# Two-layer decoder trunk on one Trainium2 core: the up product's three terms as 256-column matmuls in one PSUM region per column group

## The chip, the cores and the metric

The kernel runs on one core of one Trainium2 chip. The metric is the time of one execution in device microseconds (us); the median over several runs is given. A core has a matrix engine (TensorE, in the profile PE for matmuls and PEld for weight loads), VectorE (DVE), ScalarE (ACT), GpSimd (POOL) and SyncE (SP), which here issues the transfers. Matmuls write into PSUM; the vector and scalar engines read it from there.

## The reference

The reference computes two layers on 256 tokens of width 2048, in float32. Layer 0 mixes with a gated convolution and a spatial gate, layer 1 with attention; each layer ends with a squared-ReLU MLP of hidden width 8192, which is what the change touches:

```
def rms_norm(x, g):
    y = xf * lax.rsqrt(jnp.mean(xf * xf, axis=-1, keepdims=True) + EPS)
    return (y * g.astype(jnp.float32)).astype(x.dtype)

def channel_mlp(h, w_up, w_down):
    a = jax.nn.relu(h @ w_up)
    return (a * a) @ w_down

    h = rms_norm(x, ffn_norm[layer])
    x = x + channel_mlp(h, w_up[layer], w_down[layer])
```

## The kernel before

All weights are read once, in chunks of 512 rows by 512 columns (four k steps of 128 rows each, 1 MB). `load_chunk` takes one chunk from HBM into a `raw` tile (three of them) and splits it in two halves into a rounded part `whi` (ScalarE, L60) and a remainder `wlo` (VectorE, L61), both in a 32-bit format that TensorE streams in one pass; five buffers of each hold half chunks of two k steps. Activations are split in the same way into a high and a low half that lie side by side in one tile, `[P, G, 2, T]`: for each k step 256 high columns (the tokens), then 256 low ones. A product is the sum of three terms, high x high, high x low and low x high.

In most products (`unit`, L87) the activations are the held operand of TensorE and 512 columns of weights are streamed; two PSUM tiles with the tag "acc" collect 128 tokens each. The up product of the MLP (`unit_t`) is turned round: 128 columns of weights are held and the tokens streamed, so that the result is already transposed for the down product. For each of four column groups `f` it has one PSUM tile `up` of 512 columns, two with the tag "acc" and two with the tag "tp" (four regions for each tag). Per k step it issues four matmuls with `whi` held that stream both halves of the activations, 512 columns (L101), and then four with `wlo` held that stream the high half alone, 256 columns, into the first half of the same tile (L104). A chunk is 4 k steps, a unit is 4 chunks, 16 k steps, and gives 512 hidden columns.

`up(j)` then evacuates: for each column group ScalarE copies the second half of the tile to `r` (L348), VectorE adds the first half (L349), squares with relu two groups at a time (L350), and `split` makes the two parts of the next activation `a` (L118 on ScalarE, L119 on VectorE). The activations `h` carry the norm's gain but not 1/rms; since relu and square let a positive factor per token through, the MLP multiplies its down product by `rstd2`, the square of 1/rms (L338), when it adds it to `x` (L370).

`mlp` runs 16 up units and 16 down units per layer, in the order of 5 up, 4 down, 4 up, 4 down, 4 up, 4 down, 3 up, 4 down. Each engine works through its instructions in program order, which a scheduler lays out over the engines; a transposition of the last block of `h` stands ahead of chunk 1 of the first up unit (`pending`).

Of the kernel before, what the change touches and what calls it, by code (L numbers as in the profile page):

```python
# [9 lines left out]
F32 = mybir.dt.float32  # L10
F32R = mybir.dt.float32r
I32 = mybir.dt.int32
AF = mybir.ActivationFunctionType
ALU = mybir.AluOpType
AX = mybir.AxisListType

P = 128
T = 256
NT = T // P
D = 2048  # L20
NB = 512
G = NB // P
# [10 lines left out]
def trunk_kernel(ctx: ExitStack, tc, x, xT, vecs, sgu_gain, wsT, w_in, w_mix, w_qkv, w_ao, w_up, w_dn, out):  # L33
    nc = tc.nc
    pool = lambda name, bufs=1, **kw: ctx.enter_context(tc.tile_pool(name=name, bufs=bufs, **kw))
    const = pool("const")
# [3 lines left out]
    work = pool("work", 2)  # L40
    small = pool("small", 4)
    psum = pool("psum", 4, space=bass.MemoryType.PSUM)
# [3 lines left out]
    idle = lambda: None  # L46
# [3 lines left out]
    def load_chunk(src, first=False):  # L50
        raw = first_raw if first else raws.tile([P, G, NB], F32, name="raw")
        if not first:
            nc.sync.dma_start(raw, src)
        got = []
        for h in range(2):
            hi = parts.tile([P, 2, NB], F32R, name="whi")
            lo = parts.tile([P, 2, NB], F32R, name="wlo")
            for a, b in ((0, 1), (1, 2)) if first else ((0, 2),):
                w = raw[:, 2 * h + a:2 * h + b]
                nc.scalar.activation(hi[:, a:b], w, AF.Copy)  # L60
                nc.vector.tensor_tensor(lo[:, a:b], w, hi[:, a:b].bitcast(F32), ALU.subtract)  # L61
            got += [(hi[:, 0], lo[:, 0]), (hi[:, 1], lo[:, 1])]
        return got

    def unit(acts_t, src, order=(0, 1, 2, 3), first=False, last=False, behind=()):

        ps = [psum.tile([P, NB], F32, name=f"acc{t}", tag="acc") for t in range(NT)]
        for n, c in enumerate(order):
            if callable(acts_t[c]):
                acts_t[c] = acts_t[c]()  # L70
            chunk = load_chunk(src[c], first and n == 0)
            for later in behind[n:n + 1]:
                later()
            if n == 1 and pending:
                pending.pop()()
            ahi, alo = parts_of(acts_t[c])
            if last and n == G - 1:
                steps = [(k, t, term) for t in range(NT) for k in range(G) for term in range(3)]
            else:

                steps = [(k, t, term) for k in range(G) for term in range(3) for t in range(NT)]
            for k, t, term in steps:
                hi, lo = chunk[k]
                held, streamed = ((ahi, hi), (ahi, lo), (alo, hi))[term]
                start = n == 0 and k == 0 and term == 0
                stop = n == G - 1 and k == G - 1 and term == 2
                nc.tensor.matmul(ps[t], held[:, k, t * P:(t + 1) * P], streamed, start=start, stop=stop)  # L87
        return ps

    def unit_t(acts_t, src):  # L90

        ps = [psum.tile([P, 2, T], F32, name=f"up{f}", tag="acc" if f < 2 else "tp") for f in range(G)]
        for c in range(G):
            chunk = load_chunk(src[c])
            if c == 1 and pending:
                pending.pop()()
            both = acts_t[c]
            for k, (hi, lo) in enumerate(chunk):
                start, stop = c == 0 and k == 0, c == G - 1 and k == G - 1
                for f in range(G):  # L100
                    nc.tensor.matmul(ps[f], hi[:, f * P:(f + 1) * P], both[:, k], start=start, stop=False,  # L101
                                     skip_group_check=True)
                for f in range(G):
                    nc.tensor.matmul(ps[f][:, 0], lo[:, f * P:(f + 1) * P], both[:, k, 0], start=False, stop=stop,  # L104
                                     skip_group_check=True)
        return ps

    def act_pair(tag):

        return acts.tile([P, G, 2, T], F32R, name=tag, tag=tag, bufs=4 if tag == "h" else 5)  # L110

    def parts_of(pair):
        return pair[:, :, 0], pair[:, :, 1]

    def split(pair, at, src):

        hi, lo = parts_of(pair)
        nc.scalar.activation(hi[at], src, AF.Copy)  # L118
        nc.vector.tensor_tensor(lo[at], src, hi[at].bitcast(F32), ALU.subtract)  # L119
# [6 lines left out]
    def tps():  # L126
        return psum.tile([P, NB], F32, name="tp", tag="tp")
# [21 lines left out]
    nc.scalar.dma_start(vec, vecs)  # L149
    ident = const.tile([P, P], F32, name="ident")  # L150
    make_identity(nc, ident)
    x_sb = [const.tile([P, D], F32, name=f"x{t}") for t in range(NT)]
    wsT_sb = work.tile([P, 8, P], F32, name="wsT_sb", tag="B", bufs=1)
    sg = work.tile([P, 1024], F32, name="sg", tag="A", bufs=1)
# [20 lines left out]
    def rstd_of(ss):  # L175
        v = small.tile([P, NT], F32, name="var")
        nc.vector.tensor_reduce(v, ss, AX.X, ALU.add)
        nc.vector.tensor_scalar(v, v, 1.0 / D, EPS, ALU.mult, ALU.add)
        return rsqrt_(v, NT, "rstd")

    def norm_block(hT, j, ss, gcol):
        stats(ss, j)
        pending.append(lambda: turn_block(hT, j, gcol))
# [42 lines left out]
    def new_ss():  # L226
        return small.tile([P, NT, NJ], F32, name="ss")


    def first_block(j):  # L230
        xt = acts.tile([P, G, T], F32, name="xt", tag="a", bufs=5)
        if j == 0:
            for k in range(G):
                nc.sync.dma_start(xt[:, k], xT[:, k])  # L234
                if k == 0:
                    nc.sync.dma_start(first_raw[:, 0], w_in[2][0][:, 0])
            for k in range(1, G):
                nc.sync.dma_start(first_raw[:, k], w_in[2][0][:, k])  # L238
        else:
            nc.sync.dma_start(xt, xT[:, j * G:(j + 1) * G])  # L240
        pair = act_pair("h")
        for k in range(G):
            g = C_MIXG + j * G + k
            split_scaled(pair, k, xt[:, k], vec[:, g:g + 1])
        return pair

    hT = [lambda j=j: first_block(j) for j in range(NJ)]
    mixed_in = [None] * 4
    tail = ()
    for half in range(2):  # L250
        ps_c = unit(hT, w_in[2 + half], first=half == 0, behind=tail)
        ps_x = unit(hT, w_in[4 + half], behind=[lambda j=j: load_x(j) for j in range(NJ)] if half == 0 else ())
        if half == 0:
# [4 lines left out]
            rstd = rstd_of(ss)  # L258
# [75 lines left out]
    def mlp(layer, hT, rstd, gcol):  # L334
        aT = {}

        rstd2 = small.tile([P, NT], F32, name="rstd2")
        nc.vector.tensor_tensor(rstd2, rstd, rstd, ALU.mult)  # L338

        def up(j):  # L340

            pair = act_pair("a")
            got = unit_t(hT, w_up[layer, j])
            for half in range(2):
                r = work.tile([P, 2, T], F32, name="r")
                for f in range(2):
                    ps = got[2 * half + f]
                    nc.scalar.activation(r[:, f], ps[:, 1], AF.Copy)  # L348
                    nc.vector.tensor_tensor(r[:, f], ps[:, 0], r[:, f], ALU.add)  # L349
                nc.vector.scalar_tensor_tensor(r, r, 0.0, r, ALU.max, ALU.mult)  # L350
                split(pair, (slice(None), slice(2 * half, 2 * half + 2)), r)
            aT[j] = pair

        ss = new_ss()
        nxt = [None] * NJ
        done = 0
        for s in range(4):
            while done < min(16, 4 * s + 5):
                up(done)
                done += 1  # L360
            for j in range(NJ):
                last = s == 3 and j == NJ - 1 and gcol is None
                ps = unit([aT[4 * s + c] for c in range(4)], w_dn[layer, s, j], last=last)
                for t in range(NT):

                    w = NB // 2 if last and t == NT - 1 else NB
                    for a in range(0, NB, w):
                        cols = slice(j * NB + a, j * NB + a + w)
                        xb = x_sb[t][:, cols]
                        nc.vector.scalar_tensor_tensor(xb, ps[t][:, a:a + w], rstd2[:, t:t + 1], xb, ALU.mult, ALU.add)  # L370
                        if s == 3 and gcol is None:
                            nc.sync.dma_start(out[t * P:(t + 1) * P, cols], xb)
                if s == 3 and gcol is not None:
                    norm_block(nxt, j, ss, gcol)
        return (nxt, rstd_of(ss)) if gcol is not None else None

    hT, rstd = project(mixed_in, w_mix, (0, 2, 1, 3), C_FFNG, tail)
    hT, rstd = mlp(0, hT, rstd, C_MIXG + 16)


# [86 lines left out]
    for hg in range(4):  # L467
        got = {}
# [18 lines left out]

    hT, rstd = project(oT, w_ao, (0, 1, 2, 3), C_FFNG + 16, tail)
    mlp(1, hT, rstd, None)


# [44 lines left out]
```

## Time and profile before

| | before |
|---|---|
| median of 3 runs | 2139.3 us (2139.08 to 2139.3) |
| profiled execution | 2139.24 us |
| its span, first to last instruction | 2137.5 us |
| TensorE matmuls busy, number | 2126.9 us, 10464 |
| VectorE busy, number | 1253.8 us, 1658 |
| ScalarE busy, number | 960.9 us, 1168 |

The span is what the profiler records of the program; the execution's own time has 1.7 us around it. A busy engine is one with an instruction under way; matmuls overlap, so the sum of their durations is longer than the time that they take.

### The profile page before, as it was taken

What the parts mean: (1) busy time and instruction counts of PE and PEld (TensorE: products, weight loads), DVE (VectorE), ACT (ScalarE), POOL (GpSimd) and SP (SyncE); (2) the same over time, 40 slices, a digit from 0 to 9 for tenths busy, and PEclk for the clock granted to TensorE, in tenths of its full rate; (3) what the DMA queues carried; (4) which work ended last, traced back from release to release, by engine and by line L of the source; (5) the groups of instructions that cost most, each with busy time, mean ns of one, the idle gap of its engine ahead of it and who ended that gap; (6) DMA issues with size and microseconds to landing.
All of it is one profiled execution on the core that took longest, in us unless ns stands there. A gap on an engine that the chain in (4) does not pass through costs nothing.

```text
span 2137.5 us, 25939 instructions
## 1 busy us (share of the span) xinstructions
PE 2126.9 (100%) x10464; PEld 1795.9 (84%) x10464; DVE 1253.8 (59%) x1658; ACT 960.9 (45%) x1168; POOL 3.1 (0%) x13
## 2 busy tenths in 40 slices
PE   8999999999999999999999999999999999999999
PEld 6888888888888888888888888888888888888887
DVE  6655666655564565565666667565655554564554
ACT  5444444443443453444454555444434443443442
POOL 0000000000000000000000000000000000000000
PEclk9999999999999999999999999999999999999999
DMA  8555555555555555555545445555555555555553
GB/s 323 192 193 180 186 187 182 193 187 193 191 185 191 195 185 191 196 187 187 185 170 179 166 167 177 177 178 194 180 197 195 183 194 197 180 194 195 182 204 128
DMA packets 58584, 403.34 MB, mean 189 GB/s; under 512 B 6624, under 2 KB 7392, under 8 KB 10464
## 3 DMA queue, kind: packets, MB, share of 16 engines
q1 hardware_dynamic: 58320, 401.63, 55.0%
q8 instruction: 82, 1.34, 0.3%
q14 instruction: 38, 0.31, 0.0%
q10 hardware_dynamic: 144, 0.05, 0.0%
HBM read 399.56 MB, written 2.10 MB: 188 GB/s over the span
## 4 chain that ended last, share of the span: by engine, by line
PE 99%; DMA 0%; SPq 0%; DVE 0%; ACT 0%; issue 0%; DVEq 0%
PE acc L87 63%; PE up L101 22%; PE up L104 11%; PE tp L207 1%; PE tp L192 0%; PE tp L425 0%; DMA raw<-in_w_in 0%; PE tp L458 0%; PE tp L445 0%; PE tp L307 0%; PE tp L459 0%; SPq L234 0%; SPq L238 0%; DVE wlo L61 0%; ACT whi L60 0%
## 5 line engine op out<-in xcount | busy, mean ns | idle before, releaser
L61 DVE TENSOR_TENSOR wlo<-raw,whi 128x1024 fp32r<-128x1024 f32 (+1 forms) x754 | 919.2, 1221 | 809.3 <-ACT whi L60 808.6
L60 ACT ACTIVATE whi<-raw 128x1024 fp32r<-128x1024 f32 (+1 forms) x754 | 796.7, 1058 | 1108.3 <-PE acc L87 702.4
L87 PE MATMUL acc<-whi,a 128*128 128x512 f32 x2560 | 690.0, 390 | 0.0
L87 PEld LDWEIGHTS acc<-whi,a 128*128 128x128 f32 x2560 | 479.1, 188 | 98.2
L101 PE MATMUL up<-h,whi 128*128 128x512 f32 x2048 | 559.0, 394 | 0.0
L87 PE MATMUL acc<-wlo,a 128*128 128x512 f32 x1280 | 395.0, 389 | 0.0
L87 PE MATMUL acc<-whi,h 128*128 128x512 f32 x1408 | 386.6, 393 | 6.2 <-ACT whi L60 6.2
L101 PEld LDWEIGHTS up<-h,whi 128*128 128x128 f32 x2048 | 350.5, 189 | 47.5
L104 PEld LDWEIGHTS up<-h,wlo 128*128 128x128 f32 x2048 | 314.3, 189 | 43.6
L104 PE MATMUL up<-h,wlo 128*128 128x256 f32 x2048 | 325.8, 281 | 0.0
L87 PEld LDWEIGHTS acc<-whi,h 128*128 128x128 f32 x1408 | 263.8, 189 | 60.8 <-ACT whi L60 7.4
L87 PEld LDWEIGHTS acc<-wlo,a 128*128 128x128 f32 x1280 | 240.3, 188 | 50.4
L87 PE MATMUL acc<-wlo,h 128*128 128x512 f32 x704 | 218.3, 391 | 0.5 <-DVE wlo L61 0.5
L87 PEld LDWEIGHTS acc<-wlo,h 128*128 128x128 f32 x704 | 132.6, 188 | 28.9 <-DVE wlo L61 1.4
L370 DVE SCALAR_TENSOR_TENSOR x<-acc,rstd,x 128x512 f32<-128x512 f32 (+1 forms) x65 | 45.3, 739 | 15.8 <-PE acc L87 15.5
L349 DVE TENSOR_TENSOR r<-up,r 128x256 f32<-128x256 f32 x128 | 47.7, 414 | 0.0
L119 DVE TENSOR_TENSOR a<-r,a 128x512 fp32r<-128x512 f32 x64 | 43.7, 683 | 0.0
L350 DVE SCALAR_TENSOR_TENSOR r<-r 128x512 f32<-128x512 f32 x64 | 43.5, 680 | 0.0
L118 ACT ACTIVATE a<-r 128x512 fp32r<-128x512 f32 x64 | 39.9, 623 | 1.8
L348 ACT ACTIVATE r<-up 128x256 f32<-128x256 f32 x128 | 37.9, 380 | 0.0
L222 ACT ACTIVATE gc<-acc,rstd 128x512 f32<-128x512 f32 x28 | 17.8, 686 | 23.0 <-PE acc L87 18.6
L123 ACT ACTIVATE h<-tp,vec 128x256 fp32r<-128x256 f32 x48 | 20.5, 469 | 12.4 <-DVE h L124 12.4
(80 smaller groups left out, 383.4 us busy)
## 6 DMA issues: line engine op xcount, KB each, us to landing
raw<-in_w_up SPq DMA_DIRECT2D x128, 1024.0 KB, 4.8
raw<-in_w_dn SPq DMA_DIRECT2D x128, 1024.0 KB, 4.8
raw<-in_w_qkv SPq DMA_DIRECT2D x48, 1024.0 KB, 4.8
raw<-in_w_in SPq DMA_DIRECT2D x39, 1024.0 KB, 4.9
raw<-in_w_mix SPq DMA_DIRECT2D x16, 1024.0 KB, 4.8
raw<-in_w_ao SPq DMA_DIRECT2D x16, 1024.0 KB, 4.8
x<-in_x SPq DMA_DIRECT2D x8, 256.0 KB, 8.6
out_dram<-x SPq DMA_DIRECT2D x7, 256.0 KB, 6.1
```

Source lines behind the costliest of these rows:

```text
L60: nc.scalar.activation(hi[:, a:b], w, AF.Copy)
L61: nc.vector.tensor_tensor(lo[:, a:b], w, hi[:, a:b].bitcast(F32), ALU.subtract)
L87: nc.tensor.matmul(ps[t], held[:, k, t * P:(t + 1) * P], streamed, start=start, stop=stop)
L101: nc.tensor.matmul(ps[f], hi[:, f * P:(f + 1) * P], both[:, k], start=start, stop=False, skip_group_check=True)
L104: nc.tensor.matmul(ps[f][:, 0], lo[:, f * P:(f + 1) * P], both[:, k, 0], start=False, stop=stop, skip_group_check=True)
L118: nc.scalar.activation(hi[at], src, AF.Copy)
L119: nc.vector.tensor_tensor(lo[at], src, hi[at].bitcast(F32), ALU.subtract)
L207: nc.tensor.transpose(tp[:, i * T + t * P:i * T + (t + 1) * P], src[t][:, c:c + P], ident)
L348: nc.scalar.activation(r[:, f], ps[:, 1], AF.Copy)
L349: nc.vector.tensor_tensor(r[:, f], ps[:, 0], r[:, f], ALU.add)
L350: nc.vector.scalar_tensor_tensor(r, r, 0.0, r, ALU.max, ALU.mult)
L370: nc.vector.scalar_tensor_tensor(xb, ps[t][:, a:a + w], rstd2[:, t:t + 1], xb, ALU.mult, ALU.add)
```

## The change

Per k step the up product now issues twelve matmuls of 256 columns: `whi` held with the high half streamed, `whi` held with the low half, `wlo` held with the high half, each for the four column groups. All three terms of a column group add up in one region of 256 columns, and two groups share a PSUM tile, so a unit has two tiles with the tag "acc" and none with the tag "tp". VectorE reads a tile from PSUM once, applies relu and multiplies each column by the token's 1/rms (`rows`); ScalarE squares; `split` stays. The down product is then added to `x` without a factor. For `rows`, 1/rms has to lie along the columns in all 128 partitions: `spread` makes it once per layer, ahead of chunk 2 of the first up unit, with two copies on VectorE, two matmuls with the identity and a copy by ScalarE.

```diff
-    def unit_t(acts_t, src):
+    def unit_t(acts_t, src, behind=()):
-        ps = [psum.tile([P, 2, T], F32, name=f"up{f}", tag="acc" if f < 2 else "tp") for f in range(G)]
+        ps = [psum.tile([P, 2, T], F32, name=f"up{i}", tag="acc") for i in range(2)]
         for c in range(G):
             chunk = load_chunk(src[c])
+            for later in behind[c:c + 1]:
+                later()
             if c == 1 and pending:
                 pending.pop()()
-            both = acts_t[c]
+            xhi, xlo = parts_of(acts_t[c])
             for k, (hi, lo) in enumerate(chunk):
-                start, stop = c == 0 and k == 0, c == G - 1 and k == G - 1
-                for f in range(G):
-                    nc.tensor.matmul(ps[f], hi[:, f * P:(f + 1) * P], both[:, k], start=start, stop=False,
-                                     skip_group_check=True)
-                for f in range(G):
-                    nc.tensor.matmul(ps[f][:, 0], lo[:, f * P:(f + 1) * P], both[:, k, 0], start=False, stop=stop,
-                                     skip_group_check=True)
+                for term in range(3):
+                    held, streamed = ((hi, xhi), (hi, xlo), (lo, xhi))[term]
+                    start = c == 0 and k == 0 and term == 0
+                    stop = c == G - 1 and k == G - 1 and term == 2
+                    for f in range(G):
+                        nc.tensor.matmul(ps[f // 2][:, f % 2], held[:, f * P:(f + 1) * P], streamed[:, k],
+                                         start=start and f % 2 == 0, stop=stop, skip_group_check=True)
...
-        rstd2 = small.tile([P, NT], F32, name="rstd2")
-        nc.vector.tensor_tensor(rstd2, rstd, rstd, ALU.mult)
+        rows = work.tile([P, T], F32, name="rows", tag="C", bufs=1)
+        def spread():
+            tp = tps()
+            for t in range(NT):
+                held = work.tile([P, P], F32, name="held", tag="qT")
+                nc.vector.tensor_scalar(held, ones, rstd[:, t:t + 1], None, ALU.mult)
+                nc.tensor.matmul(tp[:, t * P:(t + 1) * P], held, ident, start=True, stop=True)
+            nc.scalar.activation(rows, tp[:, :T], AF.Copy)
...
-            got = unit_t(hT, w_up[layer, j])
+            got = unit_t(hT, w_up[layer, j], (idle, idle, spread) if j == 0 else ())
             for half in range(2):
                 r = work.tile([P, 2, T], F32, name="r")
-                for f in range(2):
-                    ps = got[2 * half + f]
-                    nc.scalar.activation(r[:, f], ps[:, 1], AF.Copy)
-                    nc.vector.tensor_tensor(r[:, f], ps[:, 0], r[:, f], ALU.add)
-                nc.vector.scalar_tensor_tensor(r, r, 0.0, r, ALU.max, ALU.mult)
+                nc.vector.scalar_tensor_tensor(r, got[half], 0.0, rows.unsqueeze(1).broadcast_to([P, 2, T]),
+                                               ALU.max, ALU.mult)
+                nc.scalar.activation(r, r, AF.Square)
                 split(pair, (slice(None), slice(2 * half, 2 * half + 2)), r)
...
-                        nc.vector.scalar_tensor_tensor(xb, ps[t][:, a:a + w], rstd2[:, t:t + 1], xb, ALU.mult, ALU.add)
+                        nc.vector.tensor_tensor(xb, ps[t][:, a:a + w], xb, ALU.add)
```

On TensorE the first k step of the first up unit stood like this before (`up_2472` to `up_2475` are the four column groups' tiles):

```order
L101 MATMUL up_2472<-h,whi 128x512
L101 MATMUL up_2473<-h,whi 128x512
L101 MATMUL up_2474<-h,whi 128x512
L101 MATMUL up_2475<-h,whi 128x512
L104 MATMUL up_2472<-h,wlo 128x256
L104 MATMUL up_2473<-h,wlo 128x256
L104 MATMUL up_2474<-h,wlo 128x256
L104 MATMUL up_2475<-h,wlo 128x256
```

After the change the same k step is this (`up_2473` and `up_2474` are the two tiles, of two column groups each; x2 are two equal rows, the two groups):

```order
L107 MATMUL up_2473<-h,whi 128x256 x2
L107 MATMUL up_2474<-h,whi 128x256 x2
L107 MATMUL up_2473<-h,whi 128x256 x2
L107 MATMUL up_2474<-h,whi 128x256 x2
L107 MATMUL up_2473<-h,wlo 128x256 x2
L107 MATMUL up_2474<-h,wlo 128x256 x2
```

Eight matmuls have become twelve, and none of 512 columns is left among them.

On ScalarE the evacuation of the first up unit stood like this before, in the midst of the conversions `whi`, with the transposed last block of `h` (L123) ahead of them:

```order
L123 ACTIVATE h<-tp,vec 128x256 x4
L60 ACTIVATE whi<-raw 128x1024 x6
L348 ACTIVATE r<-up_2472 128x256
L348 ACTIVATE r<-up_2473 128x256
L348 ACTIVATE r<-up_2474 128x256
L348 ACTIVATE r<-up_2475 128x256
L60 ACTIVATE whi<-raw 128x1024
L118 ACTIVATE a<-r 128x2x256
L60 ACTIVATE whi<-raw 128x1024
L118 ACTIVATE a<-r 128x2x256
```

Now it is this (L126 is the former L123, L121 the former L118):

```order
L126 ACTIVATE h<-tp,vec 128x256 x4
L60 ACTIVATE whi<-raw 128x1024 x2
L351 ACTIVATE rows<-tp 128x256
L60 ACTIVATE whi<-raw 128x1024 x4
L361 ACTIVATE r<-r 128x512
L121 ACTIVATE a<-r 128x2x256
L361 ACTIVATE r<-r 128x512
L121 ACTIVATE a<-r 128x2x256
L60 ACTIVATE whi<-raw 128x1024 x8
```

The copy of `rows` stands two conversions after the block of `h`, and the four operations of the evacuation stand together, ahead of the next conversion, where the conversions stood between them before.

On VectorE the start of the MLP now has the two copies among the splits of the last block of `h` (L127), ahead of five `wlo`, and then the two readings of PSUM:

```order
L143 SCALAR_TENSOR_TENSOR rstd<-rstda,rstd 128x2
L127 SCALAR_TENSOR_TENSOR h<-tp,vec,h 128x256 x2
L349 TENSOR_SCALAR held<-ones,rstd 128x128
L127 SCALAR_TENSOR_TENSOR h<-tp,vec,h 128x256 x2
L349 TENSOR_SCALAR held<-ones,rstd 128x128
L61 TENSOR_TENSOR wlo<-raw,whi 128x1024 x5
L359 SCALAR_TENSOR_TENSOR r<-up_2473,rows 128x512
L359 SCALAR_TENSOR_TENSOR r<-up_2474,rows 128x512
```

Before, the square of 1/rms (L338) stood there in place of the copies, and six `wlo` and six operations of 256 and 512 columns in place of the five and two.

## Rows read from the trace of the kernel before

**Rows 1.** The page, parts 1 and 2: engine totals, TensorE's clock by slice.

```profile
PE 2126.9 (100%) x10464; PEld 1795.9 (84%) x10464; DVE 1253.8 (59%) x1658; ACT 960.9 (45%) x1168; POOL 3.1 (0%) x13
...
PEclk9999999999999999999999999999999999999999
```

**Rows 2.** The page, part 4: the chain that ended last, shares by engine.

```profile
PE 99%; DMA 0%; SPq 0%; DVE 0%; ACT 0%; issue 0%; DVEq 0%
```

**Rows 3.** The chain in order of time: start, duration (us), what.

```profile
by line: PE acc L87 62.9%; PE up L101 22.3%; PE up L104 11.3%; PE tp L207 0.6%; PE tp L192 0.5%; PE tp L425 0.5%; DMA raw<-in_w_in 0.4%; PE tp L458 0.4%; PE tp L445 0.2%; PE tp L307 0.2%; PE tp L459 0.2%; SPq L234 0.1%; SPq L238 0.1%; DVE w
...
110.49 1.78 PE tp L307 x16
...
440.27 87.07 PE acc L87 x384
617.12 87.09 PE acc L87 x384
```

**Rows 4.** Timeline of PE, 526.9 to 531.5 us: down unit to up unit.

```profile
527.17 1.07 PE L101 MATMUL up<-h,whi 128*128 128x512 f32 x4
528.08 0.64 PE L104 MATMUL up<-h,wlo 128*128 128x256 f32 x4
528.55 1.09 PE L101 MATMUL up<-h,whi 128*128 128x512 f32 x4
529.48 0.63 PE L104 MATMUL up<-h,wlo 128*128 128x256 f32 x4
529.95 1.09 PE L101 MATMUL up<-h,whi 128*128 128x512 f32 x4
```

**Rows 5.** Timeline of PE, 326.9 to 340 us: the MLP's first up unit.

```profile
327.00 1.07 PE L101 MATMUL up<-h,whi 128*128 128x512 f32 x4
327.91 0.64 PE L104 MATMUL up<-h,wlo 128*128 128x256 f32 x4
...
333.38 1.17 PE L101 MATMUL up<-h,whi 128*128 128x512 f32 x4
334.39 0.63 PE L104 MATMUL up<-h,wlo 128*128 128x256 f32 x4
...
339.06 1.09 PE L101 MATMUL up<-h,whi 128*128 128x512 f32 x4
```

**Rows 6.** Timeline of DVE, 318 to 341 us: 1/rms and what follows.

```profile
335.25 0.15 DVE L140 SCALAR_TENSOR_TENSOR rstd<-rstda,rstd 128x2 f32<-128x2 f32 x1
...
335.71 0.15 DVE L338 TENSOR_TENSOR rstd<-rstd 128x2 f32<-128x2 f32 x1
```

**Rows 7.** Timeline of ACT, 336 to 366 us: end of the first up unit.

```profile
350.98 1.18 ACT L348 ACTIVATE r<-up 128x256 f32<-128x256 f32 x4
352.82 1.06 ACT L60 ACTIVATE whi<-raw 128x1024 fp32r<-128x1024 f32 x1 [0.66 <-PE up L101]
...
358.49 1.06 ACT L60 ACTIVATE whi<-raw 128x1024 fp32r<-128x1024 f32 x1 [1.23 <-PE up L101]
361.29 1.06 ACT L60 ACTIVATE whi<-raw 128x1024 fp32r<-128x1024 f32 x1 [1.74 <-PE up L101]
```

**Rows 8.** The page, part 5: groups, busy us, mean ns, idle before.

```profile
L370 DVE SCALAR_TENSOR_TENSOR x<-acc,rstd,x 128x512 f32<-128x512 f32 (+1 forms) x65 | 45.3, 739 | 15.8 <-PE acc L87 15.5
L349 DVE TENSOR_TENSOR r<-up,r 128x256 f32<-128x256 f32 x128 | 47.7, 414 | 0.0
L119 DVE TENSOR_TENSOR a<-r,a 128x512 fp32r<-128x512 f32 x64 | 43.7, 683 | 0.0
L350 DVE SCALAR_TENSOR_TENSOR r<-r 128x512 f32<-128x512 f32 x64 | 43.5, 680 | 0.0
L118 ACT ACTIVATE a<-r 128x512 fp32r<-128x512 f32 x64 | 39.9, 623 | 1.8
L348 ACT ACTIVATE r<-up 128x256 f32<-128x256 f32 x128 | 37.9, 380 | 0.0
```

**Rows 9.** Busy time by engine in one up unit, from the windows view.

```profile
353.30:375.70 22.40, 22.40 (x129) 19.57 (x128) 13.39 (x18) 10.68 (x15) 0.00 (x0) 1.00 0.56 190
```

More of the change, by code (lines that the diff above doesn't have):

```diff
@@ L151, in trunk_kernel @@
     make_identity(nc, ident)
+    ones = const.tile([P, P], F32, name="ones")
+    nc.vector.memset(ones, 1.0)
     x_sb = [const.tile([P, D], F32, name=f"x{t}") for t in range(NT)]
```

## The prediction

> **What bounds the kernel now.** I read the page's engine totals first: TensorE (PE) is busy for all but 10 us of the span, VectorE (DVE) for 59% of it, ScalarE (ACT) for 45%, and the clock row shows 9 in every slice, so TensorE has its upper level, 2.4 GHz, throughout [rows 1]. The chain of waits then gives 99% of the span to TensorE [rows 2]: 62.9% to the products that hold activations (L87), and 22.3% and 11.3% to the two lines of the up product, L101 and L104 [rows 3]. Nothing else holds the end. The reader should see that durations can't price a matmul here: four L104 matmuls last 0.64 us from the first start to the last end, but what comes behind them starts 0.47 us after their first [rows 4], since successive matmuls overlap. What counts is the distance from one start to the next.
>
> The chain in order of time gives that distance. Four down units, 384 matmuls of 512 columns, take 87.07 us, 226.8 ns each [rows 3]. Between the end of one such piece and the start of the next lie four up units of 16 k steps: 617.12 - (440.27 + 87.07) = 89.78 us, so a k step of the up product takes 89.78 / 64 = 1402.8 ns [rows 3]. The kernel has 2 layers x 16 units x 16 steps = 512 such steps, 718.2 us in all; the chain's shares say the same (33.6% of 2137.5 us is 718.2).
>
> The timeline splits a step. Four L101 matmuls of 512 columns start at 528.55 and the first L104 follows at 529.48; the next L101 starts at 529.95 [rows 4]: 0.93 us for four wide ones (232 ns each) and 0.47 us for four of 256 columns (118 ns each). Over the whole run, 22.3% of 2137.5 us over 2048 matmuls is 232.7 ns, and 11.3% over 2048 is 117.9 ns; with the 1402.8 ns of a step I take 118.5 for the narrow ones, from (1402.8 - 4 x 232.2) / 4.
>
> **The change, part by part.** Per k step eight matmuls (4 of 512, 4 of 256) become twelve of 256. The columns streamed stay 3072, so at 2.4 GHz the pure streaming time is 1280 ns before and after. The change removes none of it. What differs is the number of matmuls with a weight load: 8 before, 12 after, 2048 more in the kernel. So the price hangs on the start-to-start distance t of a 256-column matmul when nothing but 256-column matmuls stand around it, a stretch that the kernel before doesn't have. The time moves by 512 x (12 t - 1402.8 ns): it is even at t = 116.9 ns, and each ns of t is 6.14 us.
>
> Bounds for t. Above its streaming (213.3 ns) a 512-column matmul in the down product carries 13.4 ns [rows 3]; added to the 106.7 ns of 256 columns that makes 120.1. Among the wide ones of the up product the narrow ones now take 118.5. Even in the first step after a long run of wide matmuls, where those take (528.08 - 527.17) / 4 = 228 ns, the four narrow ones take 528.55 - 528.08 = 0.47 us, 118 each [rows 4]. So the narrow ones are not held back by the four wide ones' slower pace; they have a distance of their own. From below: half of a 226.8 ns matmul is 113.4, if the extra went with columns; and 16 short matmuls of 128 columns, each with its load, follow one another at 1.78 / 16 = 111 ns [rows 3], so loads alone can come that close. From above: the wide ones of L101 take 232.7 against 226.8 in the down product, 5.9 ns more, in steps that mix with narrow ones; if all-narrow stretches pay that on each narrow one, t is 124.4. I take the middle of the two nearest rows, 118.5 and 120.1: t = 119.3. Then a step takes 1431.6 ns, 28.8 more, and 512 of them **+14.7 us**.
>
> The Trainium skill would say otherwise: "TensorE: Matmul & The Clock Gate", section "Back-to-back issue gap", puts a warm gap at columns / 2.4 plus 2.5 ns, an estimate of 109.2 ns for 256 columns and 215.8 for 512. The trace disagrees here, 118 and 226.8 ns [rows 3, 4]; by the page's figures a step would be 1310 ns and the change -47 us, by the rows it is +14.7 us.
>
> The new broadcast of 1/rms (once per layer, ahead of chunk 2 of the first up unit) adds two matmuls of 128x128 in full float32. Nearest are the 111 ns of the short ones [rows 3]; I count each float32 product as two instructions, 4 x 111 = 0.44 us. After eight transposes the next four wide matmuls took 334.39 - 333.38 = 1.01 us against 0.91 before them [rows 5], 0.1 us more. So 0.5 us per layer, **+1.1 us** in all. Does TensorE wait for their input? 1/rms is finished on VectorE at 335.40, its square at 335.9 [rows 6]; two copies of 128x128 beside the last four splits end by about 337.6 (0.25 us each, an estimate between the 0.15 of a 2-wide and the 0.41 of a 256-wide operation [rows 6, 8]), and chunk 2 starts at 339.06 [rows 5]. That is 1.4 us in hand, so no wait. If the cover were gone, the cost would be what is late, once per layer.
>
> Behind it ScalarE must wait for the product before it copies it out, and the conversions of later chunks queue behind that copy. Five buffers let a conversion run four half chunks of 2.8 us ahead, about 11 us (the conversions come at 358.49 and 361.29, each released by TensorE [rows 7]); a wait of 1 us there is covered.
>
> The evacuation shrinks. VectorE had four additions of 0.41, two squares of 0.68 and two subtractions of 0.68 us per unit, 4.4 us; now two readings of PSUM with scale (0.74, by the add into x [rows 8]) and the subtractions, 2.8 us. ScalarE goes from four copies of 0.38 and two of 0.62 to four of about 0.62 [rows 8]: 2.8 to 2.5 us. Gain: nothing. In an up unit VectorE is busy 13.39 and ScalarE 10.68 us of 22.40 [rows 9], and both wait for TensorE. The order now puts all four ScalarE operations of a unit ahead of the next conversion, and the first of them waits for VectorE: the last ends some 0.74 + 0.74 + 2 x 0.62 + 0.6 = 3.3 us after the unit, so the conversion that started at 352.82, some 1.9 us after the first copy of PSUM at 350.98 [rows 7], comes about 1.4 us later. That too is inside the 11 us. PSUM: the four "acc" regions still serve two units in turn, and a unit of 22 us is far longer than the 1.5 us of reading, so the matmuls don't wait; the "tp" regions get free, which nobody waits for. The scalar operation in the down product becomes a plain add, under 0.1 us at the very end: 0.
>
> **Sum.** Profiled execution 2139.24 us (span 2137.5, 1.7 around it), 0.06 below the median of 2139.3: 2139.24 + 14.7 + 1.1 = **2155 us**, 0.7% slower.
>
> **The rivals.**
> The forecast's case: t from 118.5 to 120.1, that is 2150 to 2160 us. Chance 0.52.
>
> *Narrow matmuls cost in proportion to columns* (faster). In a stretch of one width the distance could settle, as the wide ones settle at 226.8, to half of it, 113.4: a step of 1361 ns, -21.5 + 1.1, 2119 us; at 111 it is 2104. It decides from t under 116 on. For it: L101 does better in pure stretches (226.8 against 232.7), and so might L104. Against it: the 118 ns in the first step after a pure stretch. The skill's 109.2 ns belongs here, and as a price it would give an estimate of 2093. Chance 0.14.
>
> *No difference:* t between 116.2 and 117.6; the saving of 5.9 ns on each wide matmul and the extra matmuls cancel. 2135 to 2143.5 us. For it: single groups of narrow ones end at 0.47 us per four, 117.5. Chance 0.10, with 0.04 for what lies between that and the forecast's case.
>
> *More than the overhead of a matmul:* loads and matmuls, 24 instructions in 1.43 us rather than 16 in 1.40, can't be delivered at this pace for 22 us on end, or the slowness of L101 goes over to all: t of 124.4 gives 1493 ns, +46.1 + 1.1, 2186 us. For it: the densest stretches that the trace shows are 16 short. Against: these run at 111 ns. Chance 0.20.
>
> **The range.** Faster by over 0.2% (4.3 us, about what a measurement of this kernel tells from no change): 0.14. Within: 0.10. Slower: 0.04 + 0.52 + 0.20 = 0.76. The range of 2138 to 2187 leaves out the faster case and a bit of the last, 0.18 together.
>
> **What would show it.** In the changed profile the k step should take 1.42 to 1.44 us, TensorE busy to within 10 us of the span as now, with 2056 more matmuls; no new wait of TensorE on ScalarE or VectorE; VectorE's busy time 45 to 55 us lower, worth nothing. The forecast is wrong if twelve narrow matmuls take under 1.40 us, or over 1.45, or if TensorE shows gaps at the unit borders or before chunk 2 of a layer's first up unit.

## The result, and the profile after

The changed kernel takes 2158.94 us (median, 2158.86 to 2158.96) against 2139.21 us before in the same comparison: a ratio of 1.0092, 95% interval 1.0075 to 1.011. It is slower by 19.7 us, as the spans of the profiled executions are: 2157.2 against 2137.5 us.

The page of the changed kernel, engine totals and clock (parts 1 and 2), answers to [rows 1]:

```profile
PE 2147.3 (100%) x12520; PEld 1906.8 (88%) x12520; DVE 1215.9 (56%) x1533; ACT 960.7 (45%) x1106; POOL 3.5 (0%) x13
...
PEclk9999999999999999999999999999999999999999
```

TensorE is still busy to within 10 us of the span, at its upper level, with 2056 more matmuls. VectorE is busy 38 us less and the kernel is slower all the same.

The changed kernel's chain in order of time (start, duration, what), against [rows 3]:

```profile
443.79 87.07 PE acc L87 x384
530.85 92.15 PE up L107 x768
623.01 87.07 PE acc L87 x384
710.07 92.15 PE up L107 x768
```

The down units are what they were, 87.07 us. Four up units between them now take 92.15 us, where 89.78 lay before: 768 matmuls of 256 columns at 120.0 ns each, a k step of 1439.8 ns against 1402.8. Eight such groups are in the kernel (512 steps of 64): 8 x 2.37 = 19.0 us, nearly the whole difference.

The rest is the broadcast. PE's timeline of the changed kernel where it stands, ahead of chunk 2 of the first up unit:

```profile
338.07 1.12 PE L107 MATMUL up<-h,whi 128*128 128x256 f32 x8
339.03 0.64 PE L107 MATMUL up<-h,wlo 128*128 128x256 f32 x4
339.51 0.60 PE L350 MATMUL tp<-ident,held 128*128 128x128 f32 x4
339.87 1.20 PE L107 MATMUL up<-h,whi 128*128 128x256 f32 x8
340.90 0.64 PE L107 MATMUL up<-h,wlo 128*128 128x256 f32 x4
```

Two products appear as four matmuls and take 339.87 - 339.51 = 0.36 us; the eight behind them take 1.03 instead of 0.96 us. That is 0.43 us a layer, 0.9 in all: 19.0 + 0.9 = 19.9 by these rows, 19.7 between the spans. VectorE's timeline of the same place shows that nothing waited for the copies:

```profile
336.05 0.28 DVE L349 TENSOR_SCALAR held<-ones,rstd 128x128 f32<-128x128 f32 x1
336.28 0.88 DVE L127 SCALAR_TENSOR_TENSOR h<-tp,vec,h 128x256 fp32r<-128x256 f32 x2
337.08 0.28 DVE L349 TENSOR_SCALAR held<-ones,rstd 128x128 f32<-128x128 f32 x1
```

The second was done at 337.36, 2.1 us before TensorE came to it.

Busy time in a stretch of an up unit, from the windows view (us of the stretch; PE, PEld, DVE, ACT, POOL with counts; clock, DMA share, GB/s), against [rows 9]:

```profile
356.00:378.00 22.00, 22.00 (x186) 22.00 (x185) 11.51 (x12) 10.06 (x12) 0.00 (x0) 1.00 0.53 193
```

The second column changed: the weight loads now fill the stretch, 22.00 of 22.00 us, where they had filled 19.57 of 22.40. That alone doesn't show that the loads hold anything up. The profile has a load at 188 to 192 ns, longer than the distance between two of them, so they overlap; in `w384` below, with 173 ns from one to the next, they fill 22 us of an up unit as well.

### The profile page after: what moved, and what is told of

Its sections match the earlier page's. It is cut to its first block, busy times and chain, and to the rows that moved or that the text cites. A ratio compares the mean times of both kernels' runs of the same rounds, so it can differ in the third digit from the quotient of the medians.

```text
span 2157.2 us, 29865 instructions
## 1 busy us (share of the span) xinstructions
PE 2147.3 (100%) x12520; PEld 1906.8 (88%) x12520; DVE 1215.9 (56%) x1533; ACT 960.7 (45%) x1106; POOL 3.5 (0%) x13
## 4 chain that ended last, share of the span: by engine, by line
PE 99%; DMA 0%; SPq 0%; DVE 0%; ACT 0%; issue 0%; DVEq 0%
PE acc L87 62%; PE up L107 34%; PE tp L212 1%; PE tp L436 0%; PE tp L197 0%; DMA raw<-in_w_in 0%; PE tp L469 0%; PE tp L456 0%; PE tp L312 0%; PE tp L470 0%; SPq L239 0%; SPq L243 0%; DVE wlo L61 0%; ACT whi L60 0%; PE tp L350 0%
## 5 line engine op out<-in xcount | busy, mean ns | idle before, releaser
L87 PE MATMUL acc<-whi,a 128*128 128x512 f32 x2560 | 689.8, 390 | 0.0
L107 PE MATMUL up<-h,whi 128*128 128x256 f32 x4096 | 575.2, 283 | 0.0
L87 PEld LDWEIGHTS acc<-whi,a 128*128 128x128 f32 x2560 | 479.1, 188 | 98.5
L107 PEld LDWEIGHTS up<-h,whi 128*128 128x128 f32 x4096 | 528.8, 192 | 0.6
L87 PE MATMUL acc<-wlo,a 128*128 128x512 f32 x1280 | 394.9, 389 | 0.0
L87 PE MATMUL acc<-whi,h 128*128 128x512 f32 x1408 | 387.1, 394 | 5.6 <-ACT whi L60 5.6
L87 PEld LDWEIGHTS acc<-whi,h 128*128 128x128 f32 x1408 | 264.3, 189 | 60.2 <-ACT whi L60 6.3
L87 PEld LDWEIGHTS acc<-wlo,a 128*128 128x128 f32 x1280 | 240.2, 188 | 50.1
L107 PEld LDWEIGHTS up<-h,wlo 128*128 128x128 f32 x2048 | 282.6, 192 | 0.0
L87 PE MATMUL acc<-wlo,h 128*128 128x512 f32 x704 | 218.7, 392 | 0.5 <-DVE wlo L61 0.5
L87 PEld LDWEIGHTS acc<-wlo,h 128*128 128x128 f32 x704 | 132.8, 189 | 28.9 <-DVE wlo L61 1.4
L359 DVE SCALAR_TENSOR_TENSOR r<-up,rows 128x512 f32<-128x512 f32 x64 | 41.2, 686 | 25.6 <-PE up L107 25.6
L381 DVE TENSOR_TENSOR x<-acc,x 128x512 f32<-128x512 f32 (+1 forms) x65 | 41.4, 678 | 15.8 <-PE acc L87 15.5
L121 ACT ACTIVATE a<-r 128x512 fp32r<-128x512 f32 x64 | 40.5, 632 | 2.0
L361 ACT ACTIVATE r<-r 128x512 f32<-128x512 f32 x64 | 39.9, 624 | 0.0
L227 ACT ACTIVATE gc<-acc,rstd 128x512 f32<-128x512 f32 x28 | 17.8, 686 | 23.0 <-PE acc L87 18.6
L126 ACT ACTIVATE h<-tp,vec 128x256 fp32r<-128x256 f32 x48 | 20.4, 469 | 12.5 <-DVE h L127 12.5
L178 DVE SCALAR_TENSOR_TENSOR junk<-x 128x512 f32<-128x512 f32 x32 | 20.9, 685 | 1.8 <-DMA x<-in_x 1.8
```

The lines of the kernel that those rows point to most:

```text
L107: nc.tensor.matmul(ps[f // 2][:, f % 2], held[:, f * P:(f + 1) * P], streamed[:, k], start=start and f % 2 == 0, stop=stop, skip_group_che ...
L126: nc.scalar.activation(hi[:, k], src, AF.Copy, scale=scale)
L178: nc.vector.scalar_tensor_tensor(junk, xb, 1.0, xb, ALU.mult, ALU.mult, accum_out=ss[:, t, j:j + 1])
L359: nc.vector.scalar_tensor_tensor(r, got[half], 0.0, rows.unsqueeze(1).broadcast_to([P, 2, T]), ALU.max, ALU.mult)
L361: nc.scalar.activation(r, r, AF.Square)
L381: nc.vector.tensor_tensor(xb, ps[t][:, a:a + w], xb, ALU.add)
```

## The experiments

The theory at the start: a 256-column matmul with its load costs 120 ns, its 106.7 ns of columns and 13.3 ns that come with each matmul, so the number of matmuls is what the change pays for. The rivals: the new evacuation or the broadcast has a part; two writes in turn to one PSUM tile hold each other up; the extra goes with the columns (one in sixteen) and the load itself binds the narrow ones.

`w512x6`, `hold64`, `stream128`, `hold32`, `w512h64` and `h64s128` were run once each, so they have no interval; the others were run four to eleven times. The kernel before stood at 2139.2 to 2139.3 us beside all of them.

**The matmuls alone** (`mm_alone`): the changed `unit_t`, but the scaling of before (`...` marks what is left out of a diff).

```diff
...
-                nc.vector.scalar_tensor_tensor(r, got[half], 0.0, rows.unsqueeze(1).broadcast_to([P, 2, T]),
-                                               ALU.max, ALU.mult)
+                nc.vector.tensor_scalar(r, got[half], 0.0, None, ALU.max)
                 nc.scalar.activation(r, r, AF.Square)
...
-                        nc.vector.tensor_tensor(xb, ps[t][:, a:a + w], xb, ALU.add)
+                        nc.vector.scalar_tensor_tensor(xb, ps[t][:, a:a + w], rstd2[:, t:t + 1], xb, ALU.mult, ALU.add)
```

> The changed kernel's matmuls alone: twelve of 256 columns per k step in two tiles, but the scaling of before (square of 1/rms in the down product, no broadcast of 1/rms, relu on VectorE and the square on ScalarE). If the number of matmuls is the cause: a k step of 1440 ns, 512 x (1440 - 1402.8) = +19.0 us against before, about 2158.2 us, 0.8 to 0.9 us under the changed kernel. If the new evacuation or the broadcast had a part beyond 0.9 us, less than that.

Measured: 2157.87 us, ratio to before 1.0088 (1.0074 to 1.0102). Its chain has the same groups:

```profile
530.03 92.15 PE up L107 x768
709.25 92.15 PE up L107 x768
```

So 18.6 of the 19.7 us come with the matmuls alone, 1.1 below the changed kernel.

**The other part alone** (`evac_alone`): the matmuls of before, with `rows`, `spread`, the square on ScalarE and the plain add.

```diff
...
-                nc.vector.scalar_tensor_tensor(r, r, 0.0, r, ALU.max, ALU.mult)
+                nc.vector.scalar_tensor_tensor(r, r, 0.0, rows.unsqueeze(1).broadcast_to([P, 2, T]),
+                                               ALU.max, ALU.mult)
+                nc.scalar.activation(r, r, AF.Square)
...
```

> The other part alone: the eight matmuls of before in four tiles, with the broadcast of 1/rms ahead of chunk 2, the scale in the relu, the square on ScalarE and the plain add in the down product. If TensorE alone sets the end: +0.9 us for the two broadcasts, about 2140.1 us, although VectorE and ScalarE have other work than before. If evacuation or broadcast matter by themselves: over 2142 us.

Measured: 2140.43 us against 2139.27, ratio 1.0007 (0.9998 to 1.0016): 1.2 us, where 0.9 was expected, and the interval does not part it from nothing. The two parts add up to the change: 18.6 + 1.2 = 19.8 us.

**PSUM tiles in turn** (`psum_order`): the changed kernel with the groups in another order.

```diff
-                    for f in range(G):
+                    for f in (0, 2, 1, 3):
```

> The changed kernel with the column groups in the order 0, 2, 1, 3, so that successive matmuls write to different PSUM tiles rather than twice to the same one. Theory 1 and the load rival: 120 ns stays, 2159 us. Rival, neighbours in one PSUM tile hold each other up: back to 118.5 ns or less, 2150 us or less.

Measured: 2158.84 us, ratio 1.0092 (1.0075 to 1.0109), the changed kernel's time. So neighbours in one PSUM tile don't hold each other up here.

**One width, the same number** (`w384`): before, with eight matmuls of 384 columns per step.

```diff
+                flat = both[:, k].rearrange("p a t -> p (a t)")
...
+                    to = ps[f].rearrange("p a t -> p (a t)")
-                    nc.tensor.matmul(ps[f], hi[:, f * P:(f + 1) * P], both[:, k], start=start, stop=False,
+                    nc.tensor.matmul(to[:, 0:384], hi[:, f * P:(f + 1) * P], flat[:, 0:384], start=start, stop=False,
...
-                    nc.tensor.matmul(ps[f][:, 0], lo[:, f * P:(f + 1) * P], both[:, k, 0], start=False, stop=stop,
+                    nc.tensor.matmul(to[:, 128:512], lo[:, f * P:(f + 1) * P], flat[:, 0:384], start=False, stop=stop,
...
```

> Eight matmuls of 384 columns per k step in place of four of 512 and four of 256: the same 3072 columns and the same number of loads as before, in one width; the low and high halves are mixed up, so the products are not those of the reference. Theory 1, a fixed 13.3 ns per matmul on top of its columns: 160 + 13.3 = 173.3 ns each, a step of 1387 ns, 8 us under before, about 2131 us. Rival, an extra that goes with the columns (one in sixteen) and a weight load of 120 ns that binds the 256-column ones: 170 ns each, a step of 1360 ns, 22 us under before, about 2117 us.

Measured: 2131.03 us, ratio 0.9961 (0.9948 to 0.9975). From its chain:

```profile
439.98 85.93 PE acc L87 x379
525.91 0.71 PE up L103 x4
...
614.68 87.08 PE acc L87 x384
```

Four up units lie between 525.91 and 614.68, 88.77 us: a step of 1387.0 ns, 173.4 for each matmul. That is 160 + 13.4, and not the 170 of an extra that goes with the columns.

**Fewer and wider** (`w512x6`): six matmuls of 512 columns per step, the same 3072 columns.

```diff
...
-                for f in range(G):
-                    nc.tensor.matmul(ps[f][:, 0], lo[:, f * P:(f + 1) * P], both[:, k, 0], start=False, stop=stop,
+                for f in range(2):
+                    nc.tensor.matmul(ps[f], lo[:, f * P:(f + 1) * P], both[:, k], start=False, stop=stop,
...
```

> Six matmuls of 512 columns per k step: the same 3072 columns, fewer loads; two column groups get their third term with the low half streamed too, two get none, so the products are not those of the reference. Both theories: 6 x 226.8 = 1361 ns per step, 21.5 us under before, about 2118 us. If the slow wide matmuls of before came from the up product itself and not from the narrow ones between them, 6 x 232.7 = 1396 ns, 2136 us.

Measured: 2116.94 us. Its chain:

```profile
436.80 87.04 PE acc L87 x384
523.84 0.91 PE up L101 x4
...
610.88 87.04 PE acc L87 x384
```

610.88 - 523.84 = 87.04 us for 64 steps, 226.7 ns a matmul, the pace of the down product. The slow wide matmuls of before (232.7 ns) were not slow by their operands: with no narrow ones among them they take 226.7.

With 3072 columns a step this makes a row of four measured steps: 6 matmuls 1360 ns, 8 of one width 1387, 12 1440, and 8 of two widths in turn 1403. The first three are 1280 ns of columns and 13.3 ns a matmul; the fourth has 16 ns on top. Every matmul in these kernels has a load of its own, so "per matmul" and "per load" can't be told apart; an order that holds the same part of `whi` for two matmuls without a second load was not tried.

**Half the load** (`hold64`): the changed kernel with 64 weight columns held.

```diff
+                        w = P if c == 0 and k == 0 else 64
-                        nc.tensor.matmul(ps[f // 2][:, f % 2], held[:, f * P:(f + 1) * P], streamed[:, k],
+                        nc.tensor.matmul(ps[f // 2][0:w, f % 2], held[:, f * P:f * P + w], streamed[:, k],
...
```

> The changed kernel with 64 weight columns held per matmul in place of 128 (all but the first k step of a unit), so half of the hidden columns are not computed; streamed columns and number of matmuls unchanged. Theory 1, a fixed 13.3 ns per matmul beside its columns: 120 ns stays, 2159 us. Rival, the load of 128 columns sets the 120 ns: with half the load the distance falls to 113 ns or less, 2118 us or less.

Measured: 2120.61 us, close to the rival's 2118. Its chain:

```profile
524.66 87.38 PE up L107 x768
699.11 87.38 PE up L107 x768
```

A unit is 21.845 us; without the 12 whole ones at 120 ns its 180 matmuls take 113.4 ns each. The 13.3 ns are not fixed: with half of the columns held, half of them is left here. The first theory falls in this form. With 64 columns held a matmul also writes 64 rows of PSUM instead of 128; no run here parts that from the load.

**Loads that bind** (`stream128`): each matmul split in two of 128 columns, each with its whole load.

```diff
+                        for half in range(2):
+                            cols = slice(half * P, (half + 1) * P)
-                        nc.tensor.matmul(ps[f // 2][:, f % 2], held[:, f * P:(f + 1) * P], streamed[:, k],
+                            nc.tensor.matmul(ps[f // 2][:, f % 2, cols], held[:, f * P:(f + 1) * P],
+                                             streamed[:, k, cols], start=start and f % 2 == 0 and half == 0, stop=stop,
...
```

> The changed kernel with each matmul of 256 columns split in two of 128, each with its load: 24 matmuls per k step, the same columns. Theory 1: 53.3 + 13.3 = 66.7 ns each, a step of 1600 ns, about 2241 us. Rival, the load binds at 109 to 120 ns: a step of 2616 to 2880 ns, 2760 to 2900 us.

Measured: 2794.07 us. Its chain:

```profile
630.13 171.47 PE up L108 x1536
888.75 171.47 PE up L108 x1536
```

111.6 ns for each, though the columns take 53.3. So a second bound exists, at 111.6 ns, just under the 120 ns of the changed kernel. The Trainium skill ("TensorE: Matmul & The Clock Gate", section "LDWEIGHTS (loading the stationary operand)") gives the time of a load in ns as its columns / 1.2, an estimate of 107 ns for 128 columns. The trace is near it, with 111.6 ns from one load to the next.

Two theories then remained for the 113.4 ns: a cost of 0.104 ns per held column (13.3 for 128), or a floor of the streaming. Two runs were to part them, and a third was to tell whether the 111.6 ns are the load or the delivery of two instructions.

**A quarter of the load** (`hold32`): `hold64` with 32 for 64.

> As the run with 64 held columns, but 32 (all but the first k step of a unit; three quarters of the hidden columns are not computed), 256 streamed. Theory now: each load takes from the matmuls 0.104 ns per held column (13.3 ns for 128, 6.7 for 64, so 3.3 for 32): 110.0 ns, about 2101 us. Rival: 113.3 ns is the streaming itself, one sixteenth over the columns, and a load of 128 only bound above it: 113.3 ns stays, about 2121 us.

Measured: 2135.11 us, more than with 64 held, which neither theory had. Its chain:

```profile
527.14 89.01 PE up L107 x768
703.22 89.01 PE up L107 x768
```

Taken as above, 115.6 ns each.

**Half the load on wide ones** (`w512h64`): `w512x6` with 64 held.

> The run of six 512-column matmuls per k step with 64 held columns (all but the first k step of a unit; half of the hidden columns are not computed). Theory now: 213.3 + 6.7 = 220.0 ns, 480 steps x 6 x 6.7 ns = 19 us less than with 128 held, about 2098 us. Rival, one sixteenth over the columns whatever is held: 226.7 ns, 2117 us.

Measured: 2126.49 us, 9.6 more than with 128 held. Its chain:

```profile
436.90 0.92 PE up L102 x4
438.29 87.04 PE acc L87 x384
526.68 0.92 PE up L102 x4
...
613.57 87.04 PE acc L87 x384
```

From 438.29 + 87.04 to 613.57 are 88.24 us; without the first step of each unit, 230 ns a matmul. Neither 220 nor 226.7: smaller loads made the wide matmuls slower. The theory of a cost per held column falls.

**Half the load on half the columns** (`h64s128`): `stream128` with 64 held.

> The run with 24 matmuls of 128 columns per k step, with 64 held columns (all but the first k step of a unit; half of the hidden columns are not computed). The 111.6 ns there were the load of 128 columns itself by the theory; half the load then leaves 53.3 + 6.7 = 60 ns, about 2200 us. Rival, the 111.6 ns are what it takes to deliver a load and a matmul to TensorE, whatever their size: 111 ns stays, about 2794 us.

Measured: 2200.24 us. Its chain:

```profile
538.46 97.07 PE up L109 x1536
722.66 97.07 PE up L109 x1536
```

A unit is 24.27 us; less 24 matmuls at 111.6 ns, 360 take 60.0 ns each. A load and a matmul are delivered every 60 ns over a hundred microseconds, so the 111.6 ns go with the 128 columns that are held, and the delivery of a load and a matmul every 120 ns held nothing up in the changed kernel.

**A better order** (`grouped`): the kernel before, with a chunk's sixteen wide matmuls first and then its sixteen narrow ones.

```diff
             for k, (hi, lo) in enumerate(chunk):
-                start, stop = c == 0 and k == 0, c == G - 1 and k == G - 1
                 for f in range(G):
-                    nc.tensor.matmul(ps[f], hi[:, f * P:(f + 1) * P], both[:, k], start=start, stop=False,
+                    nc.tensor.matmul(ps[f], hi[:, f * P:(f + 1) * P], both[:, k], start=c == 0 and k == 0, stop=False,
...
+            for k, (hi, lo) in enumerate(chunk):
+                stop = c == G - 1 and k == G - 1
                 for f in range(G):
                     nc.tensor.matmul(ps[f][:, 0], lo[:, f * P:(f + 1) * P], both[:, k, 0], start=False, stop=stop,
...
```

> The kernel before with another order within a chunk: first the sixteen wide matmuls of its four k steps, then the sixteen narrow ones. Theory: after narrow ones about ten wide ones come late, 37 ns in all, and before that is paid at each k step; once per chunk it would be 16 x 226.8 + 37 + 16 x 120 = 5586 ns against 4 x 1402.8 = 5611, 25 ns x 128 chunks, 3.2 us less: about 2136 us. Rival, the wide ones are slow beside narrow ones whatever the order: no difference, 2139 us.

Measured: 2133.2 us, ratio 0.9973 (0.9962 to 0.9983): 6.1 us less than before, where 3.2 were expected. PE's timeline in an up unit:

```profile
550.01 3.82 PE L100 MATMUL up<-h,whi 128*128 128x512 f32 x16
553.67 2.08 PE L105 MATMUL up<-h,wlo 128*128 128x256 f32 x16
555.58 3.82 PE L100 MATMUL up<-h,whi 128*128 128x512 f32 x16
```

A chunk is 5.57 us (555.58 - 550.01) against 4 x 1.4028 = 5.61: 16 wide ones in 3.66 us, 229 ns, and 16 narrow ones in 1.91 us, 119 ns. The 5586 ns that were expected had too long a delay in them. By the start times in the trace (means over the 128 chunks) only the first five wide matmuls after narrow ones come late, 27 ns in all and not 37, and the first two narrow ones after wide ones take 113.3 and 119.2 ns, 7 ns less than two of the later ones, which take 120.0.

**Half of the changes of width** (`snake`): every second chunk starts with the narrow ones.

```diff
+            for wide in ((True, False), (False, True))[c % 2]:
+                for k, (hi, lo) in enumerate(chunk):
+                    for f in range(G):
+                        if wide:
...
+                        else:
```

> The grouped order with every second chunk turned round (narrow ones first), so that wide and narrow stretches of two chunks meet and only half of the changes of width are left. Grouped has 28 ns per chunk of late wide matmuls after narrow ones (5567 against 5539 ns in a chunk that follows a down product). Theory: half of it saved, 14 ns x 128 = 1.8 us, less 0.4 us for half of the early first narrow ones: about 2131.8 us. Rival: narrow stretches twice as long keep wide ones late for longer, or the conversions come too late for chunks that start narrow: 2133 us or more.

Measured: 2131.89 us, ratio 0.9965 (0.9952 to 0.9979), as the theory had it. PE's timeline:

```profile
545.30 7.44 PE L104 MATMUL up<-h,whi 128*128 128x512 f32 x32
552.58 4.00 PE L107 MATMUL up<-h,wlo 128*128 128x256 f32 x32
556.41 7.44 PE L104 MATMUL up<-h,whi 128*128 128x512 f32 x32
```

Two chunks take 11.11 us: 32 wide ones in 7.28 us, 227.5 ns, and 32 narrow ones in 3.83, 119.7. This is the fastest kernel here that computes the products of the reference: 7.4 us under the kernel before, 27 under the changed one.

## Why the prediction was right

**What bounds the kernel.** TensorE alone, and the distance from start to start as its price: right. Taking 38 us of busy time from VectorE gave nothing, and the two parts measured apart add up to the whole.

**The price t of a narrow matmul.** Right in kind, a little short. The prediction took 119.3 ns, the middle of 118.5 (the narrow ones among wide ones) and 120.1 (the down product's 13.4 ns above streaming, put on 256 columns). Measured is 120.0, the upper of the two. The 0.7 ns are 0.7 x 6.14 = 4.3 us: the term of +14.7 us is +19.0. The row that told it is the 226.8 ns of the down product, a stretch of one width, as the changed up product is one; the 118.5 ns were of a stretch with two widths, where wide ones take about 5.5 ns longer (232.2 against 226.7) and narrow ones 1.5 ns less than by themselves. The prediction read the 118 ns of the first narrow ones after a long run of wide matmuls as "a distance of their own". They were a mean of a short passage: by the start times in the trace of before these four take 113.2, 119.0, 120.0 and 120.0 ns (means over the eight such places), so the settled 120.0 was already there, from the third on.

**The broadcast.** +1.1 us by the sum, 0.9 by the rows, 1.1 to 1.2 by the runs that have it or leave it out. The four matmuls took 0.36 us instead of 0.44, and the margin of VectorE was 2.1 us instead of 1.4.

**Covers.** The evacuation, the PSUM regions and the later conversions cost nothing, as argued: TensorE's matmuls waited 6.1 us for ScalarE and VectorE, 6.7 before, all of it in products of L87. The busy times were off, without effect: VectorE fell by 38 us, not 45 to 55, and ScalarE not at all (960.9 to 960.7), since the page's busy time counts overlapping operations once. Summed one by one, the durations in the two traces fell by 54 us on VectorE and by 8 us on ScalarE, near what was added up; four copies that were priced at 4 x 0.38 took 1.18 us together in [rows 7].

**The rivals.** Proportion to columns: refuted by the 120.0 ns and by `w384`. The Trainium skill ("TensorE: Matmul & The Clock Gate", section "Back-to-back issue gap") gives its columns / 2.4 + 2.5 ns for a single matmul taken by itself. The traces don't agree with it for this 32-bit format with a load per matmul: stretches of one width have 13.3 ns beside their columns at 256, 384 and 512. The rival of no difference had its times worked out without the broadcast's 1.1 us, which would put its t at 116.0 to 117.4 ns; nothing hangs on it. Delivery of more instructions: refuted by `h64s128`, 60 ns a pair. The slowness of L101 carried over to all (124.4 ns): it goes with the change of width, and a stretch of one width has none after its first five matmuls.

**Still open** is what the 13.3 ns are made of. With whole loads they are the same for 256, 384 and 512 columns, and depend on how many columns are held, since half of them gave 113.4 ns; but 32 held columns gave 115.6 and 64 under 512 columns 230 ns, and neither theory has both. Nor is it settled why the first wide matmuls come late after a change of width; that they do, and what it costs, the two reordered kernels show.

## What to carry to other kernels

Where TensorE sets the end, count matmuls as well as columns: here each one of 256 to 512 columns, with its load of 128, cost 13.3 ns beside its columns, so splitting a 512-column stream in two had to be paid although the rest got simpler, and work saved on engines that wait bought nothing. Take the price from a stretch that is like the new one (one width, same loads), and not from a mixed one or from the first matmuls after a change. Where two widths are needed, run each in long stretches: the order alone was worth 7.4 us here.

## What the runs showed that was not expected

Mixing widths costs by itself: eight matmuls in turn of four wide and four narrow take 1403 ns, eight of one width with the same columns 1387. Smaller loads are not always better: with 64 held columns in place of 128, matmuls of 256 columns went from 120.0 to 113.4 ns and those of 512 from 226.7 to 230; with 32 held, those of 256 columns went back to 115.6. And matmuls with a load of 128 columns each came no faster than every 111.6 ns in a long stretch, although 128 columns take 53.3, so a 256-column matmul at 120 ns is already close to that bound: the version with 128-column ones took 2794 us.
